# A 64-row form for the second row block of a mixture-of-experts expert, with the two parts of the rows side by side in one stationary operand

## The chip, the cores and the metric

One NeuronCore of a Trainium2 chip runs the whole program. The metric is the device time of one execution in microseconds (us); the kernel before has a median of 1574.97 us over three runs (1573.5 to 1577.74).

## What is computed

The reference is one decoder layer: a token mixer, a layer norm, a mixture-of-experts feed-forward part, and a layer norm. Only the third part bears on the change. Each of 1024 tokens (1024 channels wide) is sent to two of 16 experts; the rows of an expert are handled in blocks of 128:

```python
def expert_block(args):
    xb, e = args
    hid = jax.nn.silu(xb @ w_gate[e]) * (xb @ w_up[e])      # 1024 -> 512
    return hid @ w_down[e]                                  # 512 -> 1024
...
ys = lax.map(expert_block, (xs, blk_exp)).reshape(p_rows, d)
ys = ys * row_w[:, None].astype(ys.dtype)
out = jax.ops.segment_sum(ys, row_tok, num_segments=n_tok + 1)[:n_tok]
```

The number of rows of an expert depends on the data. The reference's routing, evaluated for the inputs that are timed, sends these numbers of rows to experts 0 to 15: 84, 156, 206, 90, 48, 95, 162, 151, 97, 156, 139, 306, 93, 140, 65, 60. So eight experts have more than 128 rows (1, 2, 6, 7, 9, 10, 11, 13), two of them more than 192 (2 and 11), and one more than 256 (11).

## The kernel before

All matmuls are to have nearly float32 accuracy on a datatype with fewer bits (`float32r`), so each operand is split into a high part (a rounded copy, made by ScalarE) and a low part (the rest, made by VectorE: `lo_part`). A product then takes three matmuls (`mm3`): high by high, high by low, low by high. This goes for the rows x and for every weight tile.

The experts are handled one after the other (loop over `e`). An expert has 12 weight tiles of 512 KB (8 of gate and up, 4 of down). They are loaded by the SP queue some tiles ahead into slots of a pool, and split by `e_split`, which puts one copy on ScalarE, one subtraction on VectorE and the next loads on SP. The 12 splits for expert e+1 are issued in between the steps of expert e's first block, which is the order in which each engine then works them off. Engines take their instructions in program order.

A block of 128 rows is `expert_steps`: eight `up` steps (4 products of 256 columns each, 96 matmuls in all, output `pgu`), with SiLU on ScalarE and the gating product on VectorE; two pairs of transposes of the hidden values (`tr`, output `phd`), whose result is again split into high and low; and eight `down` steps (24 matmuls of 512 columns, output `pdn`). ScalarE scales the result by the row's weight into a slot `ys`, and GpSimd adds it to the output rows with an indirect DMA (`acc_d`). The slot `ys` is kept out of reuse for a while (`held`).

The order around a loop turn e is: if the expert has more than 128 rows (a run-time branch on the count, `more`), its second block is done first with `xs[1]`, and its third (`twice`) from a third gathered tile; then comes the first block. During the first block's `down` steps, `x_prep` transposes and splits the gathered rows of expert e+1 from `xgs[0]` and `xgs[1]` into `xs[0]` and `xs[1]`; and when the first block is done, GpSimd adds its result to the output and then gathers the rows of expert e+2 into `xgs[0]` and `xgs[1]`. So at the start of turn e the tiles `xgs` are already the target of the gather for expert e+1. TensorE gets a hint for the `more` and `twice` branches (`skip_hint`), which starts the fetch of the instructions behind the likely side.

Every instruction is issued through one wrapper, so all of them carry its line number (L146) in the profile; the groups are told apart by tile names. In those, `m`, `l` and `h` are slots of the pools, and `pxe` is the output of the transposes of `x_prep`.

Of the kernel before, what the change touches and what calls it, by code (L numbers as in the profile page):

```python
# [29 lines left out]
P = 128  # L30
# [158 lines left out]
def build(ctx, tc, x, w_in, conv_w, a_log, dt_bias, onorm_g, w_br_a, w_br_b, w_o, ln1_g, ln1_b,  # L189
# [59 lines left out]
    def copy(o, i, scale=1.0):  # L249
        A.activation(o, i, AF.Copy, scale=scale)  # L250
# [9 lines left out]
            V.tensor_scalar(o, o, post, None, op0=OP.mult)  # L260


    jp = kp.tile([P, P], I32, name="jp")
# [17 lines left out]
    cidx = kp.tile([P, P], I32, name="cidx")  # L281
    G.iota(cidx, pattern=[[1, P]], base=0, channel_multiplier=0)

    lvl = []
# [18 lines left out]
    drop(ei, eq)  # L303


    xh = [new([P, S], FR) for k in range(KT)]
# [1278 lines left out]
    def x_prep(blk, half, tag, t=None):  # L1585
        h, l = xs[blk]
# [5 lines left out]
        sl = slice(4 * half, 4 * half + 4)  # L1592
        copy(h[:, sl, :], pt)
        lo_part(l[:, sl, :], pt, h[:, sl, :])

    def expert_steps(e, blk, ix, wslot, tag, fill=None, pause=-1):
        h, l = xs[blk]
        last = fill is not None
        hid, th, tl = m2.get([P, FE]), m2.get([P, 4, P], FR), m2.get([P, 4, P], FR)
        pu, py, used = {}, [], []  # L1600

        def up(fh, i, half):
            if not i and not half:
                pu[fh] = ps([P, 2, 256], name="pgu", tag=tag)
            for k in range(4 * half, 4 * half + 4):
                wh, wl = (t[:, 256 * (k % 4):256 * (k % 4) + 256] for t in ew[e, 4 * fh + 2 * i + half])
                mm3(pu[fh][:, i, :], h[:, k, :], l[:, k, :], wh, wl, k == 0, k == KT - 1)
            if last:
                used.append((e, 4 * fh + 2 * i + half))

        def silu(fh):
            A.activation(hid[:, 256 * fh:256 * fh + 256], pu[fh][:, 0, :], AF.Silu)

        def gate(fh):
            sl = slice(256 * fh, 256 * fh + 256)
            V.tensor_tensor(hid[:, sl], hid[:, sl], pu[fh][:, 1, :], op=OP.mult)

        def tr(fh):
            pt = ps([P, 2, P], name="phd", tag=tag)
            for i in range(2):  # L1620
                f = 2 * fh + i
                T.transpose(pt[:, i, :], hid[:, f * P:(f + 1) * P], ident)
            sl = slice(2 * fh, 2 * fh + 2)
            copy(th[:, sl, :], pt)
            lo_part(tl[:, sl, :], pt, th[:, sl, :])

        def down(f, half):
            if not f:
                py.append(ps([P, 512], name="pdn", tag=tag))
            sl = slice(512 * half, 512 * half + 512)  # L1630
            wh, wl = ew[e, 8 + f]
# [48 lines left out]
    def expert_block(*args):  # L1680
        steps(expert_steps(*args))

    def fills(e):
        return FIRSTF if e == 0 else LASTF if e == NE - 2 else FILLS

# [5 lines left out]
    def lists():  # L1691
        V.tensor_tensor(l2[0], l2[0], l2[1], op=OP.add)
        pt.append(ps([P, 2, 3, NE], name="pl2", tag="pb"))
        for j in range(2):
            for blk in range(3):
                T.transpose(pt[0][:, j, blk, :], l2[0][:, blk * P:(blk + 1) * P, j], ident[:NE, :NE])
        m4.free(*l2v)

    def listed():
# [73 lines left out]
    for e in range(NE):  # L1773
        col = slice(e, e + 1)
        if e + 1 < NE:
            counts.append(nc.values_load(cnt[:, e + 1:e + 2], min_val=0, max_val=S))
        c = counts[e]

        def fill():
            if e + 1 < NE:  # L1780
                e_split()

        for _ in range(12 - sum(fills(e))):
            fill()
        with tc.If(c > P, label=f"more{e}"):
            skip_hint(c, 2 * P, f"twice{e}")
            gather(idx[:, 2, col], xgs[2])
            expert_block(e, 1, idx[:, 1, col], wsl[:, 1, col], "pb")
            with tc.If(c > 2 * P, label=f"twice{e}"):
                for half in range(2):  # L1790
                    x_prep(1, half, "pb", xgs[2])
                expert_block(e, 1, idx[:, 2, col], wsl[:, 2, col], "pb")
                with tc.If(c > 3 * P):
                    with tc.For_i(3, (c + (P - 1)) // P, 1) as b:
                        lp = [tp.tile([P, 2], FT, name=f"lp{j}", tag=f"lp{j}", bufs=1) for j in range(2)]
                        for j in range(2):
                            Q.dma_start(lp[j], lst[j][bass.ds(e * S + b * P, P), :])
                        V.tensor_tensor(lp[0], lp[0], lp[1], op=OP.add)
                        li = tp.tile([P, 1], I32, name="li", tag="li", bufs=1)
                        V.tensor_copy(li, lp[0][:, 0:1])  # L1800
                        gather(li, xgs[2])
                        for half in range(2):
                            x_prep(1, half, "pb", xgs[2])
                        expert_block(e, 1, li, lp[0][:, 1:2], "pb")
# [40 lines left out]
```

## Time and profile before

| | |
|---|---|
| median of three runs | 1574.97 us (1573.5 to 1577.74) |
| the profiled execution | 1573.93 us, of which the span of the trace is 1572.2 us |
| mean granted TensorE clock | 0.971 of full speed |
| busy share: PE, VectorE, ScalarE, GpSimd | 93%, 63%, 50%, 15% |
| experts' stage | from about 1025 us to about 1542 us in the span |

The span runs from the first to the last instruction of the profiled execution; the rest of its time lies around it. A busy share is a mean over stages that are bound differently, so what the change is worth has to be read in the experts' stage alone.

### The profile page before, as it was taken

What the parts mean: (1) busy time and instruction counts of PE and PEld (TensorE: products, weight loads), DVE (VectorE), ACT (ScalarE), POOL (GpSimd) and SP (SyncE); (2) the same over time, 40 slices, a digit from 0 to 9 for tenths busy, and PEclk for the clock granted to TensorE, in tenths of its full rate; (3) what the DMA queues carried; (4) which work ended last, traced back from release to release, by engine and by line L of the source; (5) the groups of instructions that cost most, each with busy time, mean ns of one, the idle gap of its engine ahead of it and who ended that gap; (6) DMA issues with size and microseconds to landing.
All of it is one profiled execution on the core that took longest, in us unless ns stands there. A gap on an engine that the chain in (4) does not pass through costs nothing. (4 is left out here: it accounts for less than half of the span.)

```text
span 1572.2 us, 23584 instructions
## 1 busy us (share of the span) xinstructions
PE 1461.6 (93%) x8740; PEld 1271.2 (81%) x8740; DVE 989.1 (63%) x1781; ACT 781.9 (50%) x1467; POOL 241.3 (15%) x271
## 2 busy tenths in 40 slices
PE   8999999999999899999999999769999999999981
PEld 6888887888897779788888888558988989988971
DVE  6577746775567686877245447765586575527566
ACT  5545436543545555564344123445576475526554
POOL 0100001100111222121001002411122111121113
PEclk9999999999999999999999999979999999999996
DMA  6111222121202011115467447467699678748655
GB/s 207 42 38 41 64 57 65 38 64 54 68 15 61 27 48 35 28 61 167 150 207 268 154 141 198 170 208 251 191 294 330 204 215 268 222 99 256 211 165 212
DMA packets 187103, 219.83 MB, mean 140 GB/s; under 512 B 28853, under 2 KB 155877, under 8 KB 186945
## 3 DMA queue, kind: packets, MB, share of 16 engines
q1 hardware_dynamic: 164464, 176.13, 35.4%
q0 software_dynamic: 11296, 21.26, 5.8%
q10 hardware_dynamic: 11184, 20.45, 3.8%
q8 instruction: 85, 1.39, 0.4%
q14 instruction: 74, 0.60, 0.1%
HBM read 188.69 MB, written 46.68 MB: 150 GB/s over the span
## 5 line engine op out<-in xcount | busy, mean ns | idle before, releaser
L146 PE MATMUL pj<-m,m 128*128 128x512 f32 x1968 | 493.7, 399 | 2.4 <-ACT m L146 1.9
L146 DVE TENSOR_TENSOR m<-m,m 128x1024 fp32r<-128x1024 f32 (+9 forms) x336 | 364.8, 1104 | 166.7 <-ACT m L146 145.1
L146 PEld LDWEIGHTS pj<-m,m 128*128 128x128 f32 x1968 | 357.9, 189 | 70.5 <-ACT m L146 2.7
L146 ACT ACTIVATE m<-m 128x1024 fp32r<-128x1024 f32 (+2 forms) x307 | 313.0, 1049 | 128.7 <-DVE m L146 36.1
L146 PE MATMUL pgu<-m,m 128*128 128x256 f32 x1860 | 297.6, 287 | 16.0 <-DVE m L146 5.8
L146 PEld LDWEIGHTS pgu<-m,m 128*128 128x128 f32 x1860 | 264.2, 193 | 27.1 <-issue 10.4
L146 PE MATMUL pdn<-m,h 128*128 128x512 f32 x574 | 158.1, 407 | 4.2 <-ACT h L146 3.2
L146 PE MATMUL pgu<-m,l 128*128 128x256 f32 x504 | 143.8, 285 | 2.6 <-issue 2.6
L146 PEld LDWEIGHTS pdn<-m,h 128*128 128x128 f32 x574 | 100.7, 190 | 24.4 <-ACT h L146 5.8
L146 POOL TENSOR_SCALAR_AFFINE_SELECT m<-m 128x128 f32<-128x128 f32 x128 | 66.3, 538 | 288.6 <-ACT m L146 269.8
L146 DVE TENSOR_TENSOR_SCAN m<-m 128x128 f32<-128x128 f32 (+4 forms) x64 | 88.5, 1388 | 22.5 <-POOL m L146 22.3
L146 POOL DMA_INDIRECT acc_d<-m,idx x23 | 43.2, 1879 | 369.4 <-ACT m L146 164.9
L146 PEld LDWEIGHTS pgu<-m,l 128*128 128x128 f32 x504 | 98.7, 196 | 0.2 <-DVE l L146 0.2
L146 PE MATMUL pmix<-m,m 128*128 128x512 f32 x352 | 91.4, 402 | 0.0
L146 ACT ACTIVATE m<-pj 64x512 fp32r<-64x512 f32 (+2 forms) x74 | 43.8, 592 | 84.4 <-PE pj L146 61.7
L146 ACT ACTIVATE m<-pz 128x512 f32<-128x512 f32 (+2 forms) x194 | 79.9, 509 | 10.9 <-PE pz L146 5.7
L146 PE MATMUL pbr<-m,m 128*128 128x512 f32 x352 | 82.9, 390 | 0.0
L146 POOL TENSOR_TENSOR rn<-rs,mhalf 128x8 f32<-128x8 f32 x12 | 28.0, 2335 | 347.6 <-DVE rs L146 347.6
L146 PEld LDWEIGHTS pmix<-m,m 128*128 128x128 f32 x352 | 66.7, 193 | 14.3
L146 PEld LDWEIGHTS pbr<-m,m 128*128 128x128 f32 x352 | 66.0, 188 | 13.8
L146 PE MATMUL po<-h,m 128*128 128x256 f32 x320 | 55.5, 291 | 15.7 <-DVE h L146 14.6
L146 ACT ACTIVATE h<-pgu 128x256 f32<-128x256 f32 x50 | 19.2, 383 | 97.4 <-PE pgu L146 97.4
(263 smaller groups left out, 1987.9 us busy)
## 6 DMA issues: line engine op xcount, KB each, us to landing
m<-in_w_down_dram SPq DMA_DIRECT2D x63, 512.0 KB, 5.2
m<-in_w_up_dram SPq DMA_DIRECT2D x59, 512.0 KB, 8.1
m<-in_w_gate_dram SPq DMA_DIRECT2D x58, 512.0 KB, 8.1
m<-in_w_in_dram SPq DMA_DIRECT2D x45, 512.0 KB, 4.2
spill<-h ACTq DMA_DIRECT2D x40, 256.0 KB, 2.0
m<-spill SPq DMA_DIRECT2D x20, 512.0 KB, 5.0
m<-in_x_dram SPq DMA_DIRECT2D x16, 512.0 KB, 7.2
m<-in_w_o_dram SPq DMA_DIRECT2D x8, 512.0 KB, 7.8
```

Source lines behind the costliest of these rows:

```text
L146: return fn(*args, **kw)
```

## The change

The second block of an expert now has two forms. With 129 to 192 rows it is `half_block`: its 64 rows are placed with their high and their low part side by side as the 128 columns of one stationary operand, and each weight tile is passed over twice (its high and its low part), so a product takes two matmuls in place of three. The upper 64 rows of the output hold the low part's share; `both_parts` copies them down to the lower 64 partitions with ScalarE, and VectorE adds them. The hidden values are scaled by the row weight here and not at the end. The result's slot `ys` is handed back at once. With more than 192 rows the block is done as before (`whole`), but since `xs[1]` is now laid out for the 64-row form by the `x_prep` of the turn before, `x_prep` is run again at the start of the block, from `xgs[1]`, in the 128-row layout. Two constant tables move into pool slots, and some branch hints are added.

```diff
-    xs = [(m4.get([P, KT, P], FR), m4.get([P, KT, P], FR)) for _ in range(2)]
+    xs = [tuple(m4.get([P, 4, 2, P], FR) for _ in range(2)) for _ in range(2)]
...
+        parts = parts or (2 if blk and t is None else 1)
...
+        if parts == 2:
+            x_ = x_.rearrange("p k a (b r) -> p k a b r", b=2)
+            pt = pt.rearrange("p k (a r) -> p k a r", a=2)
+            h, l = x_[:, :, :, 0], x_[:, :, :, 1]
...
+    def half_block(e, ix, wslot, tag):
+        R = P // 2
...
+        def twice(pt, st, wh, wl, first, last):
+            T.matmul(pt, st, wh, start=first, stop=False)
+            T.matmul(pt, st, wl, start=False, stop=last)
...
+        def both_parts(fh, i):
+            sl = slice(256 * fh, 256 * fh + 256)
+            t = m2.get([R, 256])
+            copy(t, pu[fh][R:, i])
+            V.tensor_tensor(t, t, pu[fh][:R, i], op=OP.add)
+            if i == 0:
+                A.activation(hid[:, sl], t, AF.Silu)
+                V.tensor_scalar(hid[:, sl], hid[:, sl], wslot, None, op0=OP.mult)
+            else:
+                V.tensor_tensor(hid[:, sl], hid[:, sl], t, op=OP.mult)
...
+        for j in range(8):
+            up(j // 4, j // 2 % 2, j % 2)
+            if j % 2:
+                both_parts(j // 4, j // 2 % 2)
+            if j == 5:
+                tr(0)
+        for j, (f, half) in enumerate(DOWN):
+            down(f, half)
+            if j == 3:
+                tr(1)
+        ys = m4.get([P, D])
+        for half in range(2):
+            t, sl = m2.get([R, 512]), slice(512 * half, 512 * half + 512)
+            copy(t, py[half][R:])
+            V.tensor_tensor(ys[:R, sl], t, py[half][:R], op=OP.add)
...
+        G.indirect_dma_start(out=acc_d, ...)
+        m4.free(ys)
...
         with tc.If(c > P, label=f"more{e}"):
-            skip_hint(c, 2 * P, f"twice{e}")
-            gather(idx[:, 2, col], xgs[2])
-            expert_block(e, 1, idx[:, 1, col], wsl[:, 1, col], "pb")
...
+            skip_hint(c, 3 * P // 2, f"whole{e}")
+            with tc.If(c < 3 * P // 2 + 1, label=f"half{e}"):
+                half_block(e, idx[:P // 2, 1, col], wsl[:P // 2, 1, col], "pb")
+            with tc.If(c > 3 * P // 2, label=f"whole{e}"):
+                skip_hint(c, 2 * P, f"twice{e}")
+                gather(idx[:, 2, col], xgs[2])
+                for half in range(2):
+                    x_prep(1, half, "pb", parts=1)
+                expert_block(e, 1, idx[:, 1, col], wsl[:, 1, col], "pb")
+                with tc.If(c > 2 * P, label=f"twice{e}"):
+                    skip_hint(c, 3 * P, f"many{e}")
```

On TensorE, at the start of expert 2's second block, the order before is the branch and then the first product at once (`m18` and `m13` are the high and low rows in `xs[1]`):

```order
L146 MATMUL pdn_11231<-m32_10520,h0_11077 128x512
L1776 TENSOR_LOAD cnt_7370
L1785 COMPARE_AND_BRANCH
L1709 REGISTER_ALU
L1840 BRANCH_PREFETCH_HINT
L146 MATMUL pgu_11352<-m30_11091,m18_9630 128x256 [waits Activation_49]
L146 MATMUL pgu_11352<-m37_11093,m18_9630 128x256
L146 MATMUL pgu_11352<-m30_11091,m13_9631 128x256
```

At the same place of the change, in the `whole` form, TensorE first has the eight transposes of `xgs[1]` (`m13`):

```order
L1864 COMPARE_AND_BRANCH
L1784 REGISTER_ALU
L1922 BRANCH_PREFETCH_HINT
L146 MATMUL pxe_11770<-ident_123,m13_9456 128x128 [waits DVE_49,DMASW3_49,PE_49,Activation_49]
L146 MATMUL pxe_11770<-ident_123,m13_9456 128x128 x3
L146 MATMUL pxe_11777<-ident_123,m13_9456 128x128 [waits DVE_49,PE_49,Activation_49]
L146 MATMUL pxe_11777<-ident_123,m13_9456 128x128 x3
L146 MATMUL pgu_11787<-m22_11383,m20_9630 128x256 [waits Activation_49]
```

The first of these transposes waits for a semaphore of GpSimd's DMAs (DMASW3). On GpSimd in the change, the DMA that it stands for is the last one at the end of turn 1, behind the addition of the first block's result:

```order
L146 DMA acc_d_7363<-m4_11608,idx_9632 1152x1024 [waits DMASW2_49,DMASW3_49,DMASW1_49,DMASW5_49,DMASW0_49,Activation_49]
L146 DMA m23_9455<-h_d_7362,idx_9632 128x1024 [waits DMASW6_49,PE_49]
L146 DMA m13_9456<-h_d_7362,idx_9632 128x1024 [waits DMASW7_49]
L1851 TENSOR_LOAD cnt_7370
L1860 COMPARE_AND_BRANCH
```

On VectorE in the change, at the end of expert 1's `half_block` and the start of its first block (the third, fourth and fifth row are three of the 12 low parts for expert 2; the last row is the gating product), the slot `l0` is handed from the result to the first low part, which so waits for GpSimd's addition (DMASW0):

```order
L146 TENSOR_TENSOR l0_10817<-h4_10818,pdn_10794 64x512 [waits Activation_49]
L146 TENSOR_TENSOR l0_10817<-h2_10821,pdn_10797 64x512 [waits Activation_49]
...
L146 TENSOR_TENSOR l0_11385<-m37_10569,m22_11383 128x1024 [waits DMASW0_49,DVE_49,DMAHW5_49,PE_49,Activation_49]
L146 TENSOR_TENSOR m30_11389<-m11_10583,m0_11387 128x1024 [waits DMAHW6_49,PE_49,Activation_49]
L146 TENSOR_TENSOR m18_11405<-m27_10604,m29_11403 128x1024 [waits DMAHW7_49,PE_49,Activation_49]
L146 TENSOR_TENSOR h3_11367<-h3_11367,pgu_11370 128x256 [waits Activation_49]
```

The same handing on stands behind the half blocks of experts 6, 7, 9, 10 and 13. Before the change the slot of expert 1's second result goes to a load of a weight tile on SP (`l0_11147<-in_w_down_dram`) at the start of the first block.

## Rows read from the trace of the kernel before

**Rows 1.** The page, costliest groups: count, then busy us, mean ns, idle before.

```profile
L146 ACT ACTIVATE h<-pgu 128x256 f32<-128x256 f32 x50 | 19.2, 383 | 97.4 <-PE pgu L146 97.4
```

**Rows 2.** Timeline of PE, expert 2's second block: start us, length us, engine, operation, count.

```profile
1103.19 0.98 PE L146 MATMUL pgu<-m,m 128*128 128x256 f32 x7
...
1114.90 2.23 PE L146 MATMUL pdn<-m,h 128*128 128x512 f32 x9
...
1117.11 3.74 PE L146 MATMUL pdn<-m,h 128*128 128x512 f32 x15
1121.47 0.49 PE L146 MATMUL pgu<-m,m 128*128 128x256 f32 x2 [0.62 <-PEq L1789]
```

**Rows 3.** Window in expert 2's second block: busy PE, PEld, VectorE, ScalarE, GpSimd; clock; DMA.

```profile
1110.00:1120.00 10.00, 10.00 (x66) 8.89 (x65) 1.27 (x3) 1.63 (x4) 2.01 (x2) 1.00 0.54 134
```

**Rows 4.** Groups by line, 850 to 1572 us: small operations on ScalarE and VectorE.

```profile
L146 ACT ACTIVATE h<-phd 128x256 fp32r<-128x256 f32 x50 | 19.0, 380 | 57.2 <-PE phd L146 57.2
...
L146 DVE TENSOR_TENSOR m<-m,pbr 128x512 f32<-128x512 f32 x16 | 11.0, 685 | 16.8 <-PE pbr L146 14.1 <-ACT m L146 2.8
```

**Rows 5.** Timelines of VectorE and of PE, expert 1's first block.

```profile
1090.38 0.42 DVE L146 TENSOR_TENSOR h<-h,pgu 128x256 f32<-128x256 f32 x1 [1.03 <-ACT h L146]
1091.33 3.50 DVE L146 TENSOR_TENSOR m<-m,m 128x1024 fp32r<-128x1024 f32 x3 [0.53 <-ACT m L146]
...
1092.59 0.38 PE L146 MATMUL phd<-ident,h 128*128 128x128 f32 x2
```

**Rows 6.** Timeline of PE, expert 11: its third block's start, and the branch behind that block.

```profile
1393.02 1.03 PE L146 MATMUL pxe<-ident,m 128*128 128x128 f32 x8
1394.45 0.50 PE L146 MATMUL pgu<-m,m 128*128 128x256 f32 x2 [0.39 <-ACT m L146]
1395.17 0.39 PE L146 MATMUL pgu<-m,m 128*128 128x256 f32 x1 [0.22 <-DVE m L146]
...
1414.18 0.49 PE L146 MATMUL pgu<-m,m 128*128 128x256 f32 x2 [1.46 <-PEq L1793]
```

**Rows 7.** Timeline of all engines, end of expert 1's second block.

```profile
1083.35 0.69 ACT L146 ACTIVATE l<-pdn,wsl 128x512 f32<-128x512 f32 x1 [0.68 <-PE pdn L146]
1084.01 0.49 PE L146 MATMUL pgu<-m,m 128*128 128x256 f32 x2 [0.70 <-PEq L1789]
1084.31 1.61 POOL L146 DMA_INDIRECT acc_d<-l,idx  x1 [9.36 <-ACTq L1789]
...
1085.46 2.47 DVE L146 TENSOR_TENSOR m<-m,m 128x1024 fp32r<-128x1024 f32 x2 [4.76 <-ACT m L146]
```

**Rows 8.** DMA issues at 1084.2 to 1084.4 us: count, us from issue to landing.

```profile
acc_d<-l,idx POOLq DMA_INDIRECT x1, 4.7
```

**Rows 9.** Tile acc_d, 1060 to 1500 us, 23 indirect additions.

```profile
DMA to landing us min/median/max: 4.5/6.6/10.5
```

**Rows 10.** Timeline of GpSimd: the gathers into xgs[1] ahead of experts 2 and 11.

```profile
1110.25 1.02 POOL L146 DMA_INDIRECT m<-h_d,idx  x1 [0.31 <-issue]
...
1382.57 1.02 POOL L146 DMA_INDIRECT m<-h_d,idx  x1 [0.31 <-issue]
```

**Rows 11.** DMA issues at 1110.2 to 1110.4 us.

```profile
m<-h_d,idx POOLq DMA_INDIRECT x1, 5.5
```

**Rows 12.** DMA issues at 1382.5 to 1382.7 us.

```profile
m<-h_d,idx POOLq DMA_INDIRECT x1, 4.7
```

**Rows 13.** Timeline of PE: expert 11's second block begins.

```profile
1375.51 4.70 PE L146 MATMUL pgu<-m,m 128*128 128x256 f32 x38
```

**Rows 14.** Timeline of PE: expert 5's first block, behind a wait.

```profile
1185.22 0.78 PE L146 MATMUL pgu<-m,m 128*128 128x256 f32 x2 [2.77 <-DVE m L146]
...
1188.36 0.28 PE L146 MATMUL pgu<-m,l 128*128 128x256 f32 x1
```

**Rows 15.** Window of 5 us at that wait: columns as in rows 3.

```profile
1184.00:1189.00 5.00, 3.78 (x20) 3.79 (x21) 3.48 (x3) 3.45 (x5) 3.06 (x2) 0.66 1.10 352
```

**Rows 16.** Tile h_d: all indirect gathers of rows.

```profile
DMA to landing us min/median/max: 2.6/5.7/9.6
```

More of the change, by code (lines that the diff above doesn't have):

```diff
@@ L260, in rsqrt_ @@
             V.tensor_scalar(o, o, post, None, op0=OP.mult)
-    jp = kp.tile([P, P], I32, name="jp")
+    jp = new([P, P], I32, "jp")
     G.iota(jp, pattern=[[1, P]], base=0, channel_multiplier=-1)
@@ L280, in build @@
     G.iota(pidx, pattern=[[0, 1]], base=0, channel_multiplier=1)
-    cidx = kp.tile([P, P], I32, name="cidx")
+    cidx = new([P, P], I32, "cidx")
     G.iota(cidx, pattern=[[1, P]], base=0, channel_multiplier=0)
@@ L302, in build @@
     V.tensor_copy(bm, eq[:, 0, :].rearrange("p (b s) -> p b s", s=16)[:, :, 0])
-    drop(ei, eq)
+    drop(ei, eq, jp, cidx)
     xh = [new([P, S], FR) for k in range(KT)]
@@ L1582, in build, with x_prep @@
         Q.dma_start(l2[j].rearrange("e s c -> e (s c)"), view(lst[j], 0, [[2 * S, NE], [1, 6 * P]]))
-    xs = [(m4.get([P, KT, P], FR), m4.get([P, KT, P], FR)) for _ in range(2)]
-    def x_prep(blk, half, tag, t=None):
-        h, l = xs[blk]
+    xs = [tuple(m4.get([P, 4, 2, P], FR) for _ in range(2)) for _ in range(2)]
+    def x_prep(blk, half, tag, t=None, parts=None):
+        x_ = xs[blk][half]
+        parts = parts or (2 if blk and t is None else 1)
         t = xgs[blk] if t is None else t
@@ L1591, in x_prep @@
             T.transpose(pt[:, i, :], t[:, k * P:(k + 1) * P], ident)
-        sl = slice(4 * half, 4 * half + 4)
-        copy(h[:, sl, :], pt)
-        lo_part(l[:, sl, :], pt, h[:, sl, :])
+        if parts == 2:
[3 more added lines that the diff above has]
+        else:
+            h, l = x_[:, :, 0], x_[:, :, 1]
+        copy(h, pt)
+        lo_part(l, pt, h)
     def expert_steps(e, blk, ix, wslot, tag, fill=None, pause=-1):
-        h, l = xs[blk]
+        xb = xs[blk]
         last = fill is not None
@@ L1681, in expert_block, with up, tr, down @@
         steps(expert_steps(*args))
+    def half_block(e, ix, wslot, tag):
+        R = P // 2
+        hid, ho = m2.get([R, FE]), m2.get([P, 4, 2, R], FR)
+        pu, py = {}, []
+        def twice(pt, st, wh, wl, first, last):
+            T.matmul(pt, st, wh, start=first, stop=False)
+            T.matmul(pt, st, wl, start=False, stop=last)
+        def up(fh, i, half):
+            if not i and not half:
+                pu[fh] = ps([P, 2, 256], name="pgu", tag=tag)
+            for k in range(4 * half, 4 * half + 4):
+                wh, wl = (t[:, 256 * (k % 4):256 * (k % 4) + 256] for t in ew[e, 4 * fh + 2 * i + half])
+                twice(pu[fh][:, i, :], xs[1][half][:, k % 4, 0], wh, wl, k == 0, k == KT - 1)
+        def both_parts(fh, i):
[6 more added lines that the diff above has]
+                V.tensor_scalar(hid[:, sl], hid[:, sl], wslot, None, op0=OP.mult)
+            else:
+                V.tensor_tensor(hid[:, sl], hid[:, sl], t, op=OP.mult)
+            m2.free(t)
+        def tr(fh):
+            pt = ps([P, 2, R], name="phd", tag=tag)
+            for i in range(2):
+                f = 2 * fh + i
+                T.transpose(pt[:, i, :], hid[:, f * P:(f + 1) * P], ident[:R, :R])
+            sl = slice(2 * fh, 2 * fh + 2)
+            copy(ho[:, sl, 0], pt)
+            lo_part(ho[:, sl, 1], pt, ho[:, sl, 0])
+        def down(f, half):
+            if not f:
+                py.append(ps([P, 512], name="pdn", tag=tag))
+            sl = slice(512 * half, 512 * half + 512)
+            wh, wl = ew[e, 8 + f]
+            twice(py[half], ho[:, f].rearrange("p a b -> p (a b)"), wh[:, sl], wl[:, sl], f == 0, f == 3)
+        for j in range(8):
[13 more added lines that the diff above has]
+            V.tensor_tensor(ys[:R, sl], t, py[half][:R], op=OP.add)
+            m2.free(t)
+        m2.free(hid, ho)
+        G.indirect_dma_start(out=acc_d, out_offset=bass.IndirectOffsetOnAxis(ap=ix, axis=0),
+                             in_=ys[:R], in_offset=None, compute_op=OP.add, bounds_check=S - 1, oob_is_err=False)
+        m4.free(ys)
@@ L1694, in lists @@
         for j in range(2):
-            for blk in range(3):
-                T.transpose(pt[0][:, j, blk, :], l2[0][:, blk * P:(blk + 1) * P, j], ident[:NE, :NE])
+            for i in range(3):
+                T.transpose(pt[0][:, j, i, :], l2[0][:, i * P:(i + 1) * P, j], ident[:NE, :NE])
         m4.free(*l2v)
@@ L1785, in build @@
         with tc.If(c > P, label=f"more{e}"):
-            skip_hint(c, 2 * P, f"twice{e}")
-            gather(idx[:, 2, col], xgs[2])
-            expert_block(e, 1, idx[:, 1, col], wsl[:, 1, col], "pb")
-            with tc.If(c > 2 * P, label=f"twice{e}"):
-                for half in range(2):
[L1791 to L1804, printed above, removed]
+            skip_hint(c, 3 * P // 2, f"whole{e}")
@@ new lines, in build @@
+            with tc.If(c < 3 * P // 2 + 1, label=f"half{e}"):
[3 more added lines that the diff above has]
+                gather(idx[:, 2, col], xgs[2])
+                for half in range(2):
+                    x_prep(1, half, "pb", parts=1)
[3 more added lines that the diff above has]
+                    for half in range(2):
+                        x_prep(1, half, "pb", xgs[2])
+                    expert_block(e, 1, idx[:, 2, col], wsl[:, 2, col], "pb")
+                    with tc.If(c > 3 * P, label=f"many{e}"):
+                        with tc.For_i(3, (c + (P - 1)) // P, 1) as b:
+                            lp = [tp.tile([P, 2], FT, name=f"lp{j}", tag=f"lp{j}", bufs=1) for j in range(2)]
+                            for j in range(2):
+                                Q.dma_start(lp[j], lst[j][bass.ds(e * S + b * P, P), :])
+                            V.tensor_tensor(lp[0], lp[0], lp[1], op=OP.add)
+                            li = tp.tile([P, 1], I32, name="li", tag="li", bufs=1)
+                            V.tensor_copy(li, lp[0][:, 0:1])
+                            gather(li, xgs[2])
+                            for half in range(2):
+                                x_prep(1, half, "pb", xgs[2])
+                            expert_block(e, 1, li, lp[0][:, 1:2], "pb")
```

2 lines of the change are left out of this document (1 added, 1 removed).

## The prediction

> **What bounds the kernel now.** I read the page first: PE is busy nearly all the time, but that is an average, so I went to the experts' stage. ScalarE's SiLU operations count the blocks: 50, two for each block, so 25 blocks [rows 1]: 16 first blocks, eight second ones and one third, as the row counts of the routing say. The timeline of PE then shows one second block from end to end [rows 2]: expert 2's begins at 1103.19 without a gap, its 96 `up` matmuls last to 1114.90, its 24 `down` matmuls to 1117.11 + 3.74 = 1120.85, and the next block begins at 1121.47, behind 0.62 us that the profile puts down to the branch. So 17.66 us of back-to-back matmuls and 0.62 us of branch: 18.28 us. In such a block ScalarE and VectorE are nearly idle (1.63 and 1.27 us of 10), and the DMA engines, at half share, have room [rows 3]. PE alone bounds it, and a matmul less is time less. At the two edges of a block, however, other things set when PE goes on; there the change adds two waits.
>
> **Part 1, the 64-row form: six blocks.** By the row counts six experts take it (1, 6, 7, 9, 10, 13). It issues 64 + 16 matmuls in place of 96 + 24, of the same shapes, so 17.66 x 2/3 = 11.8 us, and 0.1 more because its four transposes don't shrink. Its last four `down` steps all need the second pair of transposes, which stands directly ahead of them; in the kernel before, three matmuls stood in between. PE waits there for transposes, a ScalarE copy and a VectorE subtraction, 0.38 + 0.38 + 0.42 us at the full size [rows 4, 5]; with half the columns the last two are shorter, so between 0.4 and 1.2 us; I take 1.0, nearer to the full size since the fixed part of small operations stays. The copying down and adding in `both_parts` runs beside `up` matmuls of the next steps. At the end the branch costs 0.62 us again [rows 2], plus one further jump: nothing if its target is already fetched, 0.84 us if it is like the jump without a hint behind expert 11's third block (1.46 against 0.62) [rows 2, 6]; the target is the next few instructions, so I take 0.2. Sum: 11.8 + 0.1 + 1.0 + 0.62 + 0.2 = 13.7 us, a saving of 4.6 us a block and **27.5 us** for six (bounds 4.0 to 5.4 a block, 24 to 32 in all).
>
> **Part 2, the slot handed on behind each 64-row block.** The first low part of the following first block is written into the slot `ys` that GpSimd's addition still reads, so VectorE waits for that DMA, and behind it, in VectorE's order, stand two more low parts, the gating product, three low parts and the split of the hidden values. In the trace [rows 7], expert 1's second block ends at 1083.31 (1084.01 less 0.70), ScalarE's last copy at 1084.04, the addition is issued at 1084.31, and VectorE's first low part starts at 1085.46. With the change an addition on VectorE (0.69 us [rows 4]) comes between copy and DMA, so the issue comes some 1.7 us behind PE's end. The landing took 4.7 us there [rows 8], with 128 rows; 64 rows could do it in half of that, 2.35, at the least, and in traffic it takes 6.6 [rows 9]. I take 4.2, close to the quiet one, since most of it need not shrink with the rows. Then the first low part starts 5.9 us behind PE's end, which is 1089.3 on the old scale in place of 1085.46. Three low parts (3.5 us) end at 1092.8, the product at 1093.2; PE asks for it at 1092.59 [rows 5], 0.6 us earlier. Three more low parts and the split bring VectorE to 1097.1. PE needs the split for its third `down` matmul: 24 `up` matmuls of 0.12 us, two transposes and two `down` matmuls of 0.24 us behind the product, at 1096.1 before and 1096.7 with the 0.6 us, so 0.4 us are added. So **1.0 us** a block, **6 us** in all. With 2.35 the product is ready by 1091.4 and costs nothing; with 6.6 it is 3.4 us a block, 20 in all.
>
> **Part 3, the 128-row form with its repeated x_prep: experts 2 and 11.** In the kernel before, PE goes from the first block's end straight into this block. Now its first instruction waits for the gather into `xgs[1]`, and GpSimd issues that gather only after ScalarE has read out the first block, after the addition into the output, and after the gather into `xgs[0]`: at 1110.25 and 1382.57 [rows 10]. They land 5.5 and 4.7 us later [rows 11, 12], at 1115.75 and 1387.27. PE had been ready at about 1103.3 and 1375.6 [rows 2, 13]. So it stands idle for 12.4 and 11.7 us; nothing else is queued on PE that could fill this, and ScalarE and VectorE have finished the splits. Then `x_prep` itself: the third block of expert 11 shows it from 1393.02 to the third matmul at 1395.17, which would have come 0.24 us behind the first without it: 1.9 us [rows 6]. And the clock: behind a wait of 2.77 us the granted clock was 0.66 over 5 us [rows 14, 15], a stretch at the lower level of 1.2 GHz: 14 matmuls took 3.14 us in place of 1.67 (the 11.71 us of the 96 `up` matmuls [rows 2] hold 98 instructions, 0.12 us each); so 1.5 us. Sum 12.05 + 1.9 + 1.5 = 15.4 us, **30.8 us** for two (bounds 28 to 34: without the clock's share, and with both landings at 6.6 us, the median of the additions [rows 9]).
>
> The Trainium skill speaks of this landing: "DMA: Bandwidth & Descriptors", section "Anatomy of one DMA — SWDGE (gpsimd) path", fits a DMA of GpSimd as about 2.0 us plus its bytes over 436 GB/s. As an estimate from that page, a gather of 512 KB lands in 3.2 us, and 256 KB in 2.6; the sum would be some 10 us less than mine, about the time before. The rows, 5.5 and 4.7 us, disagree for these gathers, and what is measured decides; what the page would bring is rival (a).
>
> **Part 4, the rest.** The new hint ahead of the third-block branch may bring expert 11's 1.46 us down to 0.62 [rows 2, 6]: -0.8. The constants' new slots and the new layout in `x_prep` keep the count and size of every operation ahead of the experts' stage: 0, covered by nothing but their being the same work. SP's loads go on behind the additions as before.
>
> **Sum.** The profiled execution took 1573.93 us (span 1572.2), 1.0 below the median. 1573.9 - 27.5 + 6 + 30.8 - 0.8 = 1582.4, so about **1583** as a median.
>
> **Rivals.**
> (a) GpSimd's DMAs land fast: the additions of 64 rows in 2.35 us and a little more, so that VectorE's wait is hidden (6 us less), and the two gathers in 2.6 us, the fastest of all 40 (5 us less [rows 16]): 1572. For it: half the rows of an addition, in a quiet stretch; and the gathers ahead of experts 2 and 11 fetch the second blocks of experts 3 and 12, which have 90 and 93 rows and so none there. Against it: it was so before too, and they landed in 5.5 and 4.7 us; no addition landed in under 4.5 [rows 9].
> (b) The addition lands late, as the median of 6.6 us: PE stands 3.4 us a block, 14 us more: 1597. For it: SP's loads restart at about that time. Against it: the quiet 4.7 [rows 8].
> (c) Faster: the gather's wait is not on PE's path, because the program order leaves it done before the block begins. Then the two blocks cost 1.9 us each, and the time is 1583 - 27 = 1556. It decides from an entry cost of under some 8 us a block on. For it: `xgs[1]` is requested a whole block ahead for the `x_prep` of the other turns. Against it: here it is asked for directly behind the request.
> (d) The 64-row form is taken by fewer blocks: 1583 + 4 a block. The counts nearest to a limit are 139, 162 and 206, so this is nearly excluded.
>
> **How the numbers follow.** My case has 0.55, (a) 0.18, (b) 0.14, (c) 0.11, (d) 0.02. My case's own range is 1576 to 1591 (bounds of parts 1 and 3). Between two medians of this kernel 0.3%, 4.7 us, is about what can be told from no change, so "same" is 1570.3 to 1579.7. Of my case 0.44 is slower and 0.11 same; (a) is same for 0.13, faster for 0.05; (b) and (d) are slower; (c) is faster. That makes 0.16 faster, 0.24 same, 0.60 slower. The range that leaves out 2 in 10 drops (c) and the far end of (b): 1569 to 1597.
>
> **What would show it.** Six gaps of 13 to 14 us between a second block's first matmul and the next block's; in two places PE idle for about 12 us ahead of `pxe`, released by the DMA from `h_d`, with a lower granted clock behind it; VectorE idle at the start of six first blocks, released by the DMA into `acc_d`, and PE idle by about 1 us ahead of the first `phd` there. Wrong would make me: a gather that lands in 2 to 3 us behind fewer requests, VectorE's wait going under or growing to 3 us, or a jump behind the 64-row form that costs over 1 us.

## The result, and the profile of the changed kernel

The changed kernel takes 1654.75 us (median of four runs, 1653.24 to 1659.58), the kernel before 1574.72 us in the same series (four runs, 1573.5 to 1577.74): 1.051 times as long, with an interval of 1.048 to 1.054. The direction is as forecast, but not the size: +80 us where I had written +8.

The two profiled executions have spans of 1651.8 and 1572.2 us, 79.6 us apart. GpSimd issues one addition into the output (`acc_d`) at the end of every block but the last (expert 15's), so its timeline cuts the experts' stage into blocks. For the block of expert 3, which has 90 rows and so no second block, it reads in the kernel before (start us, length us, engine, operation, then in brackets the idle time ahead of it and what ended it):

```profile
1143.97 2.07 POOL L146 DMA_INDIRECT acc_d<-m,idx  x1 [20.51 <-ACTq L1785]
...
1164.12 2.11 POOL L146 DMA_INDIRECT acc_d<-m,idx  x1 [14.52 <-ACTq L1785]
```

and in the changed kernel:

```profile
1162.42 2.04 POOL L146 DMA_INDIRECT acc_d<-m,idx  x1 [20.65 <-ACTq L1860]
...
1192.04 2.12 POOL L146 DMA_INDIRECT acc_d<-m,idx  x1 [24.87 <-ACTq L1860]
```

Before, expert 2's first block ends at 1143.97, and expert 3's ends 20.15 us later; in the changed kernel expert 3's ends 29.62 us behind expert 2's. All 24 additions, taken so and summed by kind ("the rest" goes on from the last of them to the span's end):

| from one addition to the next, us | before | after | difference | forecast |
|---|---|---|---|---|
| span's start to expert 0's addition | 1069.31 | 1072.86 | +3.6 | 0 |
| six 64-row blocks (1, 6, 7, 9, 10, 13) | 91.75 | 90.93 | -0.8 | with the next row |
| the first blocks behind these | 132.95 | 137.97 | +5.0 | -21.5 (27.5 less 6) |
| second blocks of 2 and 11 | 30.67 | 61.88 | +31.2 | +30.8 |
| six turns without a second block (3, 4, 5, 8, 12, 14) | 131.47 | 170.64 | +39.2 | 0 |
| the rest | 116.05 | 117.52 | +1.5 | -0.8 |

The forecast's sum was +8.5, so 71 us are missing, and 65 of them are in two places: the 64-row form with the block behind it saves nothing (+4.2 where -21.5 was forecast), and blocks in which not one instruction of the 64-row form runs take 6.5 us more each.

**The 64-row form.** TensorE, expert 1's 64-row block and the start of the block behind it:

```profile
1069.19 2.06 PE L146 MATMUL pgu<-m,m 128*128 128x256 f32 x16
1073.49 4.09 PE L146 MATMUL pgu<-m,m 128*128 128x256 f32 x32 [2.24 <-DVE h L146]
1077.51 0.33 PE L146 MATMUL phd<-ident,h 64*128 64x64 f32 x2
1078.56 2.17 PE L146 MATMUL pgu<-m,m 128*128 128x256 f32 x16 [0.71 <-DVE h L146]
...
1083.53 2.11 PE L146 MATMUL pdn<-m,h 128*128 128x512 f32 x8 [0.69 <-DVE h L146]
1086.32 1.69 PE L146 MATMUL pgu<-m,m 128*128 128x256 f32 x12 [0.69 <-DVE l L146]
```

From 1069.19 to 1086.32 it is 17.13 us, where [rows 2] give 18.28 and I forecast 13.7. The matmul count is as forecast (64 and 16). New are two waits of 2.24 and 0.71 us, each ahead of the product of the up weights: TensorE waits there until VectorE has read the gate product. VectorE's rows show why it is late: it still works on three splits of the block before.

```profile
1069.57 3.50 DVE L146 TENSOR_TENSOR m<-m,m 128x1024 fp32r<-128x1024 f32 x3
1073.02 0.41 DVE L146 TENSOR_TENSOR h<-h,pgu 64x256 f32<-64x256 f32 x1
...
1091.24 1.23 DVE L146 TENSOR_TENSOR l<-m,m 128x1024 fp32r<-128x1024 f32 x1 [4.27 <-DMA acc_d<-l,idx]
1092.38 2.35 DVE L146 TENSOR_TENSOR m<-m,m 128x1024 fp32r<-128x1024 f32 x2
1094.66 0.41 DVE L146 TENSOR_TENSOR h<-h,pgu 128x256 f32<-128x256 f32 x1
```

The third row is the wait that Part 2 forecast, at its place: the addition is issued at 1087.25, the low part starts 3.99 us later. At experts 6, 7, 9 and 10 the same wait ends 3.8 to 4.4 us behind the addition.

**The blocks without a second block.** VectorE and TensorE, expert 3's block. In the kernel before, the first low parts of this block start 1.01 us behind the addition (1143.97), and TensorE does not wait at its first transposes:

```profile
1144.98 3.50 DVE L146 TENSOR_TENSOR m<-m,m 128x1024 fp32r<-128x1024 f32 x3 [0.39 <-ACT m L146]
...
1150.19 0.38 PE L146 MATMUL phd<-ident,h 128*128 128x128 f32 x2
```

In the changed kernel:

```profile
1171.65 2.36 DVE L146 TENSOR_TENSOR m<-m,m 128x1024 fp32r<-128x1024 f32 x2 [8.62 <-DMA acc_d<-l,idx]
...
1175.53 0.69 PE L146 MATMUL phd<-ident,h 128*128 128x128 f32 x2 [5.03 <-DVE h L146]
```

VectorE's first low part waits 8.62 us, until 9.2 us after the addition of expert 2's block, though no 64-row block has run in this turn; TensorE then stands for 5.03 us, and behind that its granted clock is at the lower level of 1.2 GHz (columns as in [rows 3]), which is part of what the block loses:

```profile
1175.50:1180.50 5.00, 4.97 (x24) 4.97 (x25) 4.85 (x5) 1.88 (x3) 0.00 (x0) 0.50 0.99 349
```

The list of VectorE's waits has ten for an addition (us in total, times, longest):

```profile
DVE m L146 <- DMA acc_d<-m,idx: 42.3, 7, 9.2
DVE m L146 <- DMA acc_d<-l,idx: 16.1, 2, 8.6
DVE l L146 <- DMA acc_d<-l,idx: 4.3, 1, 4.3
```

By VectorE's timeline five of them stand behind a 64-row form (4.1 to 4.7 us, experts 1, 6, 7, 9, 10) and five in turns without a second block (7.4 to 9.2 us, experts 3, 5, 8, 12, 14). At expert 4 VectorE waits 7.3 us at the same place, but the profile names another DMA.

**The second blocks of experts 2 and 11.** TensorE at expert 2, and GpSimd's gather into `xgs[1]` ahead of it:

```profile
1117.95 1.94 PE L146 MATMUL pxe<-ident,m 128*128 128x128 f32 x8 [11.73 <-DMA m<-h_d,idx]
...
1113.13 1.02 POOL L146 DMA_INDIRECT m<-h_d,idx  x1 [0.31 <-issue]
```

The window of 5 us behind the wait (columns as in [rows 3]):

```profile
1118.00:1123.00 5.00, 5.00 (x22) 4.54 (x23) 1.39 (x2) 1.19 (x2) 0.00 (x0) 0.50 0.23 90
```

TensorE's wait is 11.73 us (11.52 at expert 11), against the forecast 12.4 and 11.7, and behind it the granted clock is 0.50, the lower level of 1.2 GHz.

### The profile page after: what moved, and what is told of

Its sections match the earlier page's. It is cut to its first block, busy times and chain, and to the rows that moved or that the text cites. A ratio compares the mean times of both kernels' runs of the same rounds, so it can differ in the third digit from the quotient of the medians.

```text
span 1651.8 us, 23338 instructions
## 1 busy us (share of the span) xinstructions
PE 1460.0 (88%) x8516; PEld 1263.8 (77%) x8516; DVE 1008.9 (61%) x1833; ACT 793.4 (48%) x1495; POOL 229.7 (14%) x265
## 5 line engine op out<-in xcount | busy, mean ns | idle before, releaser
L146 PE MATMUL pgu<-m,m 128*128 128x256 f32 x1416 | 208.5, 302 | 33.1 <-DVE h L146 17.5
L146 PEld LDWEIGHTS pgu<-m,m 128*128 128x128 f32 x1416 | 193.4, 207 | 44.2 <-DVE h L146 19.6
L146 PE MATMUL pdn<-m,h 128*128 128x512 f32 x530 | 150.0, 412 | 11.2 <-DVE h L146 6.3
L146 PEld LDWEIGHTS pdn<-m,h 128*128 128x128 f32 x530 | 94.1, 193 | 30.7 <-DVE h L146 9.9
L146 PE MATMUL pgu<-m,l 128*128 128x256 f32 x732 | 107.9, 296 | 0.0
L146 ACT ACTIVATE h<-pgu 128x256 f32<-128x256 f32 (+1 forms) x62 | 23.7, 382 | 116.6 <-PE pgu L146 105.8
L146 PE MATMUL pxe<-ident,m 128*128 128x128 f32 x280 | 45.2, 291 | 32.0 <-DMA m<-h_d,idx 23.2
```

The source lines that it names most:

```text
L146: return fn(*args, **kw)
```

## The experiments

The block times below are sums of the same kind as in the table, from each kernel's profiled execution, so each is a single reading. "Single blocks" are the six turns without a second block: 131.47 us before, 170.64 us changed.

**k1_hold: the slot held.** The result's slot is kept out of reuse as in the other forms.

```diff
-        m4.free(ys)
+        held.append((epos[1] + HOLD, ys))
```

> The result slot of the 64-row form is held back for four splits, as the other forms hold theirs, in place of being free at once; nothing else. Theory (slot): in the changed kernel the first low part of every following first block is written into that slot, and VectorE waits there for GpSimd's DMAs even where the 64-row form is not taken, behind the addition and the two gathers of the turn before. Then the six blocks of experts with up to 128 rows (3, 4, 5, 8, 12, 14) lose their 39 us, and the six first blocks behind a 64-row form some 5: about 1610. Rival (branch): these blocks are slow because of the nested branches and the longer code that is jumped over; then only the 5 us go: about 1650. Rival (slots): another order of slots makes SP's loads late; also about 1650.

Measured: 1621.64 us (1.0311, interval 1.0275 to 1.0347), 33 us less than the changed kernel. The single blocks take 139.53 us (31.1 less), the first blocks behind a 64-row block 133.27 (4.7 less). Of VectorE's ten waits one short one is left:

```profile
DVE m L146 <- DMA acc_d<-m,idx: 1.3, 1, 1.3
```

The branch rival falls for what went: branches and code are those of the changed kernel. The slot theory gets 31 of its 39 us and 33 of its 45 in all; 8 stay in these blocks. The largest single wait among these is TensorE's 5.09 us ahead of expert 5's first block, which the profile puts down to the branch (L1860; 0.38 to 0.44 us at experts 3, 4, 12 and 14); in the kernel before that place has 2.77 us behind VectorE [rows 14]. Why it is longer is open.

**k2_copy: no gather to wait for.** The rows of the 128-row form are copied from the other layout.

```diff
-                for half in range(2):
-                    x_prep(1, half, "pb", parts=1)
+                x1, x2 = xs[1], tuple(m4.get([P, 4, 2, P], FR) for _ in range(2))
+                for half in range(2):
+                    x_ = x1[half].rearrange("p k a (b r) -> p k a b r", b=2)
+                    o_ = x2[half].rearrange("p k b (a r) -> p k b a r", a=2)
+                    copy(o_[:, :, 0], x_[:, :, :, 0])
+                    V.tensor_copy(o_[:, :, 1], x_[:, :, :, 1])
+                xs[1] = x2
...
+                xs[1] = x1
+                m4.free(*x2)
```

> Ahead of the second block with more than 192 rows, the rows are put from the 64-row layout into the 128-row layout by copies within the SBUF (ScalarE the high parts, VectorE the low parts, into two free slots), in place of x_prep from the gathered tile; nothing else. Theory (gather): TensorE's 11.6 us at the start of experts 2 and 11 are the landing of the gather and go; it then waits only for the copies, which come behind the splits on ScalarE and VectorE, about 4.5 us in place of 15.5: 22 us less, about 1633. Rival: the branch and the code of the longer form make the wait; then no more than 4 us are gained, 1650.

Measured: 1599.14 us (1.0158, 1.0124 to 1.0193), 56 us less. The two blocks take 42.14 us in place of 61.88, 19.7 less, as the gather theory says; TensorE's wait there is down to two of 4.0 us, for which the profile names VectorE's sequencer at the branch of the 64-row form (k8_gather has the same without the copies). The other 36 us were not expected, and they are in blocks that the edit does not touch: the single blocks take 141.38 us (29.3 less), the first blocks behind a 64-row block 129.95 (8.0 less). The two slots that are taken and given back shift the list of free slots: in the program's order the slot of the 64-row result now goes to the result of the loop for more than 384 rows, and only from there to a split, the fifth low part of the first block in place of the first. This second, unintended edit of who gets the slot speaks for the slot theory as well.

**k3_tiles: a PSUM tile for each product.**

```diff
-            if not i and not half:
-                pu[fh] = ps([P, 2, 256], name="pgu", tag=tag)
+            if not half:
+                pu[fh, i] = ps([P, 256], name="pgu", tag=tag)
...
-            copy(t, pu[fh][R:, i])
-            V.tensor_tensor(t, t, pu[fh][:R, i], op=OP.add)
+            copy(t, pu[fh, i][R:])
+            V.tensor_tensor(t, t, pu[fh, i][:R], op=OP.add)
```

> In the 64-row form gate and up product get a PSUM tile each in place of the halves of one; nothing else. Theory (tile): TensorE waits in each 64-row form 2.3 and 0.7 us ahead of the up product because VectorE has not yet read the gate product out of the same tile; both waits go, 2.9 us x 6 = 17 us, about 1637. Rival (backlog): VectorE and ScalarE are still busy with the splits of the block before, so the wait only moves on to the first transposes, and less than 6 us are gained: about 1650.

Measured: 1631.78 us (1.0376, 1.034 to 1.0412), 23 us less. TensorE in expert 1's 64-row block:

```profile
1067.63 5.90 PE L146 MATMUL pgu<-m,m 128*128 128x256 f32 x48
1073.55 0.34 PE L146 MATMUL phd<-ident,h 64*128 64x64 f32 x2
...
1078.79 2.11 PE L146 MATMUL pdn<-m,h 128*128 128x512 f32 x8 [0.69 <-DVE h L146]
1081.53 1.69 PE L146 MATMUL pgu<-m,m 128*128 128x256 f32 x12 [0.63 <-DVE l L146]
```

Both waits are gone, and the block takes 13.90 us. The six take 69.14 us in place of 90.93. The backlog rival falls: VectorE reads the first product here at 1071.47, when TensorE is in the middle of 48 matmuls.

**k4_all: the three together.**

> The three edits together. If the three theories hold and their gains add up (45, 22 and 17 us): about 1571, at or under the kernel before (1574.7). Rival: with VectorE and TensorE freed, the loads of the weights (SP, 12 x 512 KB an expert) bound the turns with one block, and no more than half of the 17 and 22 us comes through: about 1590.

Measured: 1569.52 us (ten runs; 0.9978 of the kernel before, 0.9963 to 0.9994). The sum of the three forecasts (84 us) came, 85 us; its terms did not. Alone the three edits gave 33, 56 and 23 us, 112 in sum, where 45, 22 and 17 were forecast; at once they give less, since k1 and k2 each take some 30 us out of the same single blocks. What it still loses against the kernel before is 4.5 us in the single blocks (136.00) and 11.7 us at experts 2 and 11 (42.41); the six 64-row blocks (69.13) are 22.6 us shorter than the blocks they replace. At expert 2 TensorE waits 3.99 us, and its first 12 matmuls then take 3.07 us in place of 1.68 (the same group at the start of the first block behind), at a granted clock of 0.50 (second row, columns as in [rows 3]):

```profile
1105.76 3.07 PE L146 MATMUL pgu<-m,m 128*128 128x256 f32 x12 [3.99 <-DVEq L1862]
...
1105.76:1108.80 3.04, 3.04 (x13) 2.94 (x14) 0.91 (x2) 0.22 (x1) 2.43 (x3) 0.50 0.52 63
```

**k8_gather: one gather less in some turns.** It would have fetched no row.

```diff
-            for blk in range(2):
+            for blk in range(1 if e + 2 in (3, 4, 5, 8, 12, 14, 15) else 2):
                 gather(idx[:, blk, e + 2:e + 3], xgs[blk])
```

> The changed kernel, with the gather into the second tile left out at the end of those turns where the expert that it fetches for has up to 128 rows (3, 4, 5, 8, 12, 14, 15), so that it would have fetched no row; nothing else. Theory (slot): where the 64-row form is not taken, VectorE's wait ends when all of GpSimd's DMAs ahead of the branch have landed, the gathers too; so the first blocks of experts 3, 4 and 14, which stand behind a gather that is gone, end their wait some 1.3 us earlier each, and those of 5, 8 and 12 do not change. Theory (gather): TensorE's waits of 11.6 us at experts 2 and 11 go, since no gather into the tile is under way, about 13 us each with the clock. Sum about 1625. Rival: VectorE waits for the addition alone; then 3, 4 and 14 stay as they are, and it is 1629. Rival (branch) for experts 2 and 11: nothing changes there, 1650.

Measured: 1617.72 us (1.0295, 1.0271 to 1.032). Experts 2 and 11 take 46.52 us (15.4 less, where some 26 were expected: TensorE still waits 3.98 us there). At expert 2 this wait ends at 1108.76, right behind VectorE's last splits of the block before (1106.21 + 2.35); the profile names VectorE's sequencer at the branch of the 64-row form, where VectorE raises the semaphores of the form that is skipped. In the single blocks both sides were wrong: those of experts 3, 4 and 14 do not get 1.3 us shorter but 8.1, 5.3 and 6.8; that of 5 gets 4.4 longer, and 8 and 12 stay (28.76 and 28.18). So it is not the landing of one gather more or less; with one DMA less in the turn before, these three blocks (21.53, 22.54 and 22.72 us) are near their length in the kernel before (20.15, 21.51 and 22.87).

The theory that I formed on this: what matters is the number of GpSimd's DMAs. They report on eight semaphores in turn (DMASW0 to 7), and each place in the program has its fixed one. Where a branch is not taken, GpSimd raises the semaphores of the DMAs in it itself, and the order shows what it waits for first (the `ISA` row raises them). In the changed kernel, at expert 1 (the addition of the block before reports on DMASW5: the next addition waits for it):

```
242 L146 DMA acc_d_7363<-l0_10817,idx_9632 1152x1024 [waits DMASW5_49,DMASW0_49,DVE_49]
270 L1860 ISA [waits DMASW3_49,DMASW4_49,DMASW2_49,DMASW5_49,DMASW1_49,DMASW0_49]
```

The branch now has six DMAs in place of five (two of them in the loop for more than 384 rows), and the sixth shares its semaphore with the addition of the block just before. Before all six are raised, that addition must have landed; and VectorE's low part, which asks for the 64-row form's semaphore, waits with it.

**k9_lanes: five DMAs again.** The gather in the loop for more than 384 rows is left out; the inputs never enter that loop.

```diff
-                            gather(li, xgs[2])
```

> The changed kernel without the gather in the loop for more than 384 rows, a branch that these inputs never enter; so GpSimd has five DMAs in the branch of the second block in place of six, as the kernel before has, and no instruction that runs is removed. Theory (lanes): GpSimd's DMAs report on eight semaphores in turn; where the branch is not taken, GpSimd itself raises those of the DMAs in it, after waiting for the earlier DMA on each of them. With six of them one is that of the addition of the block just before, with five it is not. VectorE's wait for the slot then goes in the blocks of experts 3, 4, 5, 8, 12 and 14, some 31 to 35 us, and stays in the six behind a 64-row form: about 1621. Rival (slot alone): the slot that is handed on makes the wait whatever the number of DMAs: 1654, no change.

In the order of this kernel the same two rows read:

```
241 L146 DMA acc_d_7363<-l0_10814,idx_9632 1152x1024 [waits DMASW5_49,DVE_49]
268 L1860 ISA [waits DMASW3_49,DMASW2_49,DMASW4_49,DMASW1_49,DMASW0_49]
```

Measured: 1618.28 us (1.028, 1.0255 to 1.0305), 36 us less than the changed kernel, by leaving out an instruction that never runs. The single blocks take 136.11 us (34.5 less), the first blocks behind a 64-row block 137.16 (0.8 less), as the theory says: where the 64-row form runs, VectorE waits for that form's own addition still. The slots are handed out as in the changed kernel, so another order of slots (k1's third rival) is not the cause of these 34.5 us. At expert 3 the wait of 8.62 us is one of 2.58:

```profile
1165.75 2.36 DVE L146 TENSOR_TENSOR m<-m,m 128x1024 fp32r<-128x1024 f32 x2 [2.58 <-DMA acc_d<-l,idx]
```

**b1_free, b2_lanes, b3_both: the same on the kernel before.** These have no 64-row form. b1 frees the slots of second and third blocks at once, b2 writes the never-entered gather twice, b3 does both.

```diff
-        held.append((epos[1] + HOLD, ys))
+        if blk:
+            m4.free(ys)
+        else:
+            held.append((epos[1] + HOLD, ys))
...
+                        gather(li, xgs[2])
                         gather(li, xgs[2])
```

> The kernel before, with the result slot of second and third blocks free at once in place of held back for four splits; nothing of the 64-row form. Theory (slot): a slot that GpSimd still reads is handed on here too, in every turn, to a load or a split at the start of the first block; the blocks of experts 3, 4, 5, 8, 12 and 14 get longer, by 1 to 5 us each, since here it goes mostly to loads of SP and not to the first low part: about 1590. Rival: without the 64-row form the handing on costs nothing: 1574.

> The kernel before with the gather in the loop for more than 384 rows, never entered, written twice, so that the branch of the second block has six DMAs of GpSimd in place of five; nothing that runs is added. Theory (lanes): the semaphores are raised late in the turns without a second block here too, and whoever has taken a held slot waits: SP's loads, by as much as in the changed kernel with the slot held, 8 us in the six blocks together: about 1580. Rival: the number of DMAs does nothing by itself: 1573.

> The kernel before with both: slots of second and third blocks free at once, and six DMAs of GpSimd in the branch in place of five. Theory: the two together make the wait that each alone does not; since the slots go to splits and loads at the start of the first block here, 10 to 30 us: about 1593. Rival: as with the slots alone, 1576.

Measured: b1 1575.93 us (1.0021, 1.0006 to 1.0037), so its rival was right to some 3 us; b2 1582.88 us (1.0045, 1.0029 to 1.0062), near its theory's 1580, though only 4.1 of the 8 us that it put into these blocks are there; b3 1616.49 us (1.0256, 1.0234 to 1.0278), above what I expected. The single blocks:

| single blocks, us | slot held | slot free at once |
|---|---|---|
| before, five DMAs in the branch | 131.47 | 130.42 (b1) |
| before, six DMAs | 135.55 (b2) | 170.33 (b3) |
| 64-row form, six DMAs | 139.53 (k1) | 170.64 (the change) |
| 64-row form, five DMAs | - | 136.11 (k9) |

b3's blocks come within 0.3 us of the change's, without one line of the 64-row form. Here it is ScalarE that was given the third block's slot, for a high part, and waits until 9.4 us after the addition of the block before (1146.44; the profile names a gather that lands then); TensorE follows:

```profile
1155.83 2.00 ACT L146 ACTIVATE m<-m 128x1024 fp32r<-128x1024 f32 x2 [8.43 <-DMA m<-h_d,idx]
...
1159.67 0.69 PE L146 MATMUL phd<-ident,h 128*128 128x128 f32 x2 [6.84 <-DVE h L146]
```

So neither cause does it alone: the slot decides that an engine with work for TensorE asks for the semaphore early, the sixth DMA that it is raised late.

**k6_best, k7_tr, k10_best8: towards a faster kernel.** k6 is k4_all with the two constant tables back in their own places. k7 adds the transposes one step earlier. k10 is k6 without the never-entered gather, so it does not cover an expert with more than 384 rows.

```diff
         for j, (f, half) in enumerate(DOWN):
             down(f, half)
-            if j == 3:
+            if j == 2:
                 tr(1)
```

> The kernel with the three edits (slot held, a PSUM tile each, copies in place of x_prep), and the two constant tables back where they were before the change. The experts' stage then starts earlier: expert 0's first block ended 2.8 us later than in the kernel before with the three edits, 3.5 us with the change alone. Theory (the tables' slots shift the loads there): 3 us less, 1566.5. Rival (the layout of xs or the order of loads does it): no change, 1569.5.

> As the kernel with the tables back, and the second pair of transposes in the 64-row form one step earlier, so that one down step (two matmuls, 0.5 us) stands behind them while ScalarE and VectorE split the result. Theory: of the 0.7 us of TensorE's wait there 0.5 us go, in six blocks 3 us: 1563.5. Rival: the hidden values are not ready one step earlier, and the wait moves ahead of the transposes: no change.

> The kernel with the three edits and the tables back, and without the gather in the never-entered loop (five DMAs in the branch). Theory: the turns without a second block lose the rest of what they cost over the kernel before, 2 us together, and SP's loads start earlier: about 1567. Rival: with the slot held nobody waits for those semaphores any more, 1569.5.

Measured: k6 1569.58 us (0.9983, 0.9968 to 0.9998), no different from k4_all, as its rival said; expert 0's addition comes at 1071.46, where k4_all has 1072.06. k7 1570.71 us (0.9989, 0.9975 to 1.0004): the 64-row blocks do get shorter, 67.05 us in place of 69.16 for six, but the first block behind expert 13's took 24.57 us in this profile in place of 21.65 (TensorE stands 2.04 us at the jump there, see the last section), and the total cannot be told from k6. k10 1563.35 us (0.9925, 0.9909 to 0.994), the fastest, 4 us under its theory: its single blocks take 125.74 us in place of 133.42.

## Why the prediction was wrong

**Part 1 failed at one sentence**: that the copying down and adding in `both_parts` "runs beside `up` matmuls of the next steps". The next steps write the other half of the same PSUM tile (2 x 256 float32, 2 KB a partition), and the program makes TensorE wait until both readers are through: 2.24 + 0.71 us. With that gone (k3_tiles) the block takes 13.90 us, 0.2 from the forecast 13.7, so the rest of the working held in this block. (The lower bound of the saving was mis-added: the part's own terms give 3.7 us a block, not 4.0. Its 0.2 us for the further jump failed at experts 9 and 10, as said under Part 2.) In the six blocks the waits cost more than 2.95 us each (21.8 us in all went with them): behind the first one the 32 matmuls took 5.60 us at expert 10 and 5.59 at expert 13, in place of 4.09, at a lower granted clock (last section). The changed program's order would have told: the up product has its own wait for VectorE. The Trainium skill has the rule on its page "PSUM — Partial Sum Buffer", section "PSUM bank collisions raise a hardware error": accesses are to be kept apart by semaphores "by bank × quadrant", not by address, so two halves of one bank count as one. The trace agrees as far as it goes: the program guards the whole tile, and TensorE goes on at 1073.49, right behind VectorE's read (1073.02 + 0.41). No run here lets the two overlap.

**Part 2 came near where it looked and was blind elsewhere.** At the six blocks it forecast +6 us, and +5.0 were measured; the addition of 64 rows held VectorE for 3.8 to 4.4 us where I took 4.2. That the sums agree is in part luck: 2.4 and 2.7 of the 5.0 us are at experts 9 and 10, where the jump out of the 64-row form took 2.00 and 2.34 us in place of the 0.62 + 0.2 of Part 1, and the other four blocks are within 0.4 us of what they were. The slot's own share is what k1_hold takes away, 4.7 us. (In its working, 1083.31 + 5.9 is 1089.2 and not 1089.3.) The failed step is the count: "behind each 64-row block". A slot is handed on in the program, so the wait for it stands in every turn, and in the turns that skip the branch its semaphore has to be raised by someone. I put that at nothing, without a reason; it and the clock behind it are most of the 39.2 us in six blocks, the largest term of all (k1_hold takes 31.1 us of them away, k9_lanes 34.5). k1, k9 and the pair b1 and b3 show both halves of the cause. Rival (b), a landing of 6.6 us for 64 rows, was not it.

**Part 3 held**: +31.2 us for two blocks, forecast 30.8. k2_copy and k8_gather show that the gather ends the wait, so rival (c) falls. A wait that Part 3 did not have lies under it: without the gather TensorE still waits 4.0 us for VectorE at the 64-row form's branch (k8_gather, k4_all).

**Part 4**: the hint's 0.8 us came (expert 11's first block 22.98 to 22.26). The start of the experts' stage did not stay as it was: +3.6 us. Putting the tables back did not settle it, and b1_free, which changes nothing ahead of the experts, has expert 0's addition at 1065.71. These shifts of a few us stay unexplained; each is one profiled execution, and whole executions of the kernel before spread from 1565.46 to 1577.85 us in one series, so none is shown to come from an edit.

## What to carry to other kernels

A wait that a program carries for the sake of a branch is also there when the branch is skipped: for every tile that passes from inside a branch to outside, ask who raises its semaphore on the other path, and behind what. Count the DMAs inside a branch: here the 64-row form's own addition made them six, and leaving out another one, never executed, gave 36 us back. And when two products share a PSUM tile, their readers stand between their writers.

## What was not expected of the hardware

- Between the last matmul of the 64-row form and the next block's first, TensorE stood for 0.63 to 0.69 us at four experts, but for 2.00 us at expert 9 and 2.34 at expert 10, by the same sequence of instructions; there the profile names TensorE's sequencer at the jump, and the granted clock behind it was 0.66 over 5 us (third row, for expert 9, columns as in [rows 3]; it was 0.66 at expert 10 too and 1.00 at expert 1). Such a wait of 2.0 to 3.1 us comes back at both experts in k1_hold, k3_tiles and k9_lanes, at one expert in k8_gather (10) and k7_tr (13), and nowhere in k2_copy, k4_all, k6_best and k10_best8. Why is open.

```profile
1364.09 1.09 PE L146 MATMUL pgu<-m,m 128*128 128x256 f32 x7 [2.00 <-PEq L1864]
1405.15 1.90 PE L146 MATMUL pgu<-m,m 128*128 128x256 f32 x12 [2.34 <-PEq L1864]
...
1364.00:1369.00 5.00, 4.91 (x28) 4.92 (x29) 1.49 (x2) 1.85 (x3) 1.18 (x1) 0.66 0.53 125
```

- A wait of TensorE of some 2.3 us in the 64-row form was in two of six blocks followed by 32 matmuls at 0.175 us each (5.60 / 32), in the others at 0.128 us (4.09 / 32). The granted clock shows the difference: over the 4 us behind the wait it was 0.57 and 0.63 at experts 10 and 13, and 1.00 at the four others. Why the same wait was followed by the lower level only twice is open. Experts 10 and 9:

```profile
1389.20:1393.20 4.00, 4.00 (x20) 4.00 (x21) 0.34 (x1) 0.69 (x2) 3.15 (x3) 0.57 0.65 86
...
1350.00:1354.00 4.00, 3.98 (x32) 3.88 (x32) 1.18 (x3) 0.79 (x2) 3.16 (x3) 1.00 0.56 78
```
